# Feed-forward gate and up tiles: one 512-column matmul for two products, corrections summed apart

## The chip, the cores and the metric

The kernel runs on one core of a Trainium2 chip. The metric is the device time of one execution in microseconds. Three runs of the kernel before gave 1154.39 to 1155.62 us, with a median of 1154.85 us. One further execution was profiled; all rows and durations below come from it.

## The reference

Five stages follow each other on a sequence of 256 tokens with 1,024 channels, in float32: two hybrid layers (a gated recurrence, gated linear attention and sparse attention side by side), a feed-forward stage, a mixing stage, and a second feed-forward stage. The change touches the feed-forward stages alone:

```python
def swiglu(x, w_gate, w_up, w_down):
    return (jax.nn.silu(x @ w_gate) * (x @ w_up)) @ w_down

h = h + 0.5 * swiglu(rmsnorm_2(h, ffn1_norm[l]), ffn1_w_gate[l], ffn1_w_up[l], ffn1_w_down[l])
...
h = h + 0.5 * swiglu(rmsnorm_2(h, ffn2_norm[l]), ffn2_w_gate[l], ffn2_w_up[l], ffn2_w_down[l])
```

`w_gate` and `w_up` are 1024 x 2816, `w_down` is 2816 x 1024.

## The kernel before

TensorE multiplies in a reduced form of float32 (`F32R`). To keep the accuracy of float32, each operand is split into a rounded part and its remainder, `hi` and `lo`, and a product is the sum of three: hi by hi, hi by lo and lo by hi. `mm3` (lines 136 to 141) issues these three matmuls into one PSUM region.

The weights come as 362 units of 128 x 1024 values (512 KB), in the order of their use. `weights()` (lines 101 to 114) issues the DMA of a unit into `raw` (3 buffers), casts it to `hi` on ScalarE (line 112) and subtracts on VectorE to get `lo` (line 113); `hi` and `lo` have 5 buffers each. These steps get a high priority, so they stand in their engines' queues as far ahead of the matmuls as the buffers allow.

The activations of a stage, normed and transposed to 128 channels x 8 tiles x 256 tokens, are split in the same way. `norm()` makes two tiles for them, `xh` and `xl`, which `split` (lines 131 to 134) fills.

A projection reads a unit in one of two ways. `proj_a` holds x as the stationary operand and moves 512 columns of weights; its result has tokens on the partitions. `proj_b` (lines 173 to 182) holds 128 x 128 of the weights and moves the 256 tokens; its result has channels on the partitions. For each unit it takes the eight channel tiles `k` in turn and calls `mm3`: 24 matmuls of 256 columns. With n = 2 two units fill one PSUM bank, `ps[:, 0]` and `ps[:, 1]`.

`ffn()` makes the first 512 of the 2,816 hidden channels by `proj_a`, and the other 2,304 in nine turns of `j` (lines 858 to 863). A turn is `g = proj_b("fg")`, `u = proj_b("fu")`, four units in all, then `gated`: a tanh on ScalarE (line 839, tile `fth`), two multiplications on VectorE (lines 841 and 842, tile `fs`), and a split into `hh` and `hl` (lines 133 and 134). `out_proj` multiplies `hh` and `hl` by `w_down` (tiles `op`, 512 columns each).

The PSUM pool `pj` has four banks in rotation, for all projections and for the four accumulators of `out_proj`. A scheduler sets the order on each engine from the order of the program and the priorities; each engine works through its own queue in that order.

Of the kernel before, what the change touches and what calls it, by code (L numbers as in the profile page):

```python
# [8 lines left out]
F32R = mybir.dt.float32r  # L9
U8 = mybir.dt.uint8  # L10
AF = mybir.ActivationFunctionType
ALU = mybir.AluOpType
# [3 lines left out]
P = 128  # L16
S = 256
D = 1024
KT = D // P
# [14 lines left out]
class Net:  # L34
# [138 lines left out]
    def proj_b(self, x, name, n=2):  # L173
# [7 lines left out]
            self.tick()  # L181
        return ps

    def rsqrt(self, out, v, scale, eps, post=None):

        n = v.shape[-1]
        g = self.nc.gpsimd
        g.tensor_scalar(out, v, scale, eps, ALU.mult, ALU.add)
        g.tensor_tensor(out, out, self.mhalf[:, :n], ALU.pow)
        if post is not None:  # L190
            g.tensor_scalar(out, out, post, None, ALU.mult)
# [58 lines left out]
    def norm(self, g_src):  # L250


        g = self.row_bc(g_src, D, "g_bc")
        xh = self.big.tile([P, KT, S], F32R, tag="xh", name="xh")
        xl = self.big.tile([P, KT, S], F32R, tag="xl", name="xl")

        def fill(t):
            with self.tc.high_priority(self.ahead(2 * LEAD)):
                halves = self.normed(t, g)

            def turn():
                for b, xs in enumerate(halves):
                    ps = self.transposes([xs[:, P * k:P * (k + 1)] for k in range(4)], "xT")
                    ks, ts = slice(4 * b, 4 * b + 4), slice(P * t, P * (t + 1))
                    with self.tc.high_priority(self.ahead(2 * LEAD)):
                        self.split(xh[:, ks, ts], xl[:, ks, ts], ps)

            return turn

        return (xh, xl), fill  # L270
# [559 lines left out]
    def ffn(self):  # L830

        nc = self.nc
        x = self.xn
        hh = self.work([P, 22, S], "hh", dtype=F32R)
        hl = self.work([P, 22, S], "hl", dtype=F32R)

        def gated(g, u, n):
            th = self.tmp([P, n], "fth")
            nc.scalar.activation(th, g, AF.Tanh, scale=0.5)
            s = self.tmp([P, n], "fs")  # L840
            nc.vector.scalar_tensor_tensor(s, th, 1.0, g, ALU.add, ALU.mult)
            nc.vector.tensor_tensor(s, s, u, ALU.mult)
            return s

        def transposed(t, s):
            yield
            yield
            tp = self.transposes([s[:, P * i:P * (i + 1)] for i in range(4)], "hT")
            ts = slice(P * t, P * (t + 1))
            self.split(hh[:, 0:4, ts], hl[:, 0:4, ts], tp)  # L850

        gs = []
        self.proj_a(x, "fg", lambda t, ps: gs.append(ps))
        us = self.proj_a(x, "fu")
        for t in range(2):
            self.start(transposed(t, gated(gs[t], us[t], 512)))
        f = lambda z: z.rearrange("p a b -> p (a b)")
        for j in range(9):
            g = self.proj_b(x, "fg")
            u = self.proj_b(x, "fu")  # L860
            s = gated(f(g), f(u), 512)
            ks = slice(4 + 2 * j, 6 + 2 * j)
            self.split(f(hh[:, ks, :]), f(hl[:, ks, :]), s)
        self.join()
        self.out_proj((hh, hl), 22, 0.25)
# [195 lines left out]
def layouts(np, ins):  # L1061
# [31 lines left out]
    def ffn(n):  # L1093
# [4 lines left out]
        return out + rows(wd, range(0, DFF, 256))  # L1098

    units += ffn(1)  # L1100
    w = g("w_in_2")[0]
    units += pa(w, 1024) + pb(w, 0, 1024) + pa(w, 2048) + pa(w, 1536) + pb(g("w_gate_2")[0], 0, 2048)
    for n in ("attn", "gmlp"):
        wb = g(f"w_branch_{n}_2")[0]
        units += [tiles(wb[:, c:c + 256]) for c in range(0, 1024, 256)]
    units += rows(g("w_out_2")[0], range(0, 1024, 256))
    units += ffn(2)

    cols = np.zeros((P, NCOLS), f)
# [70 lines left out]
```

## Time and profile before

| What | Value |
|---|---|
| Median of 3 runs | 1154.85 us |
| Profiled execution | 1154.77 us |
| its span, first to last instruction | 1153.1 us |
| TensorE busy | 1131.9 us, 98% |
| VectorE busy | 776.5 us, 67% |
| ScalarE busy | 590.5 us, 51% |
| Mean granted clock of TensorE | 0.998 |
| Feed-forward stages, turns of j | 624.4 to 728.9 us and 981.8 to 1086.3 us |

The span is the time between the first and the last instruction; the execution is 1.7 us longer. In the rows, PE is TensorE's matmuls, PEld its loads of stationary operands, DVE is VectorE, ACT is ScalarE. The length that a matmul is shown with (283 ns for 256 columns) is a modelled one with its way through the array; matmuls follow each other at a shorter distance, so what one costs is read from the distance of their starts. "L141" is line 141 of the kernel, and `fg<-xh,hi` names the tile written and the tiles read, with buffer numbers left out. Behind "idle before" stands what ended an engine's idle time in front of an instruction.

### The profile page before, as it was taken

What the parts mean: (1) busy time and instruction counts of PE and PEld (TensorE: products, weight loads), DVE (VectorE), ACT (ScalarE), POOL (GpSimd) and SP (SyncE); (2) the same over time, 40 slices, a digit from 0 to 9 for tenths busy, and PEclk for the clock granted to TensorE, in tenths of its full rate; (3) what the DMA queues carried; (4) which work ended last, traced back from release to release, by engine and by line L of the source; (5) the groups of instructions that cost most, each with busy time, mean ns of one, the idle gap of its engine ahead of it and who ended that gap; (6) DMA issues with size and microseconds to landing.
All of it is one profiled execution on the core that took longest, in us unless ns stands there. A gap on an engine that the chain in (4) does not pass through costs nothing.

```text
span 1153.1 us, 18080 instructions
## 1 busy us (share of the span) xinstructions
PE 1131.9 (98%) x7114; PEld 1010.1 (88%) x7114; DVE 776.5 (67%) x1138; ACT 590.5 (51%) x854; POOL 92.4 (8%) x133
## 2 busy tenths in 40 slices
PE   8999999999999999999999999999999999999997
PEld 5888789898798888989878999888989997999986
DVE  5697896886668879678656656546495477656543
ACT  5645745554464675456445444435564445444432
POOL 1111111121011210112100000000020000000000
PEclk9999999999999999999999999999999999999999
DMA  8846555556564654455656566666653665666662
GB/s 271 258 144 201 156 159 156 152 170 179 173 205 148 199 148 142 139 161 166 183 163 222 178 183 184 189 194 203 189 175 105 184 191 179 188 183 183 186 197 74
DMA packets 59309, 203.57 MB, mean 177 GB/s; under 512 B 6668, under 2 KB 9620, under 8 KB 59224
## 3 DMA queue, kind: packets, MB, share of 16 engines
q1 hardware_dynamic: 59224, 202.42, 58.1%
q8 instruction: 56, 0.92, 0.3%
q14 instruction: 29, 0.24, 0.1%
HBM read 201.20 MB, written 2.11 MB: 176 GB/s over the span
## 4 chain that ended last, share of the span: by engine, by line
PE 88%; DVE 6%; DMA 2%; ACT 1%; issue 1%; POOL 0%; SPq 0%; DVEq 0%; POOLq 0%; ACTq 0%
PE op L141 19%; PE fg L141 11%; PE fu L141 11%; PE gatep L141 4%; PE mk L141 4%; PE mq L141 4%; PE mz L141 4%; PE mv L141 3%; PE mo L141 3%; DVE lo L113 2%; PE brp L141 2%; PE qk2p L141 2%; PE dz L141 2%; PE dv L141 2%; DMA raw<-in_w 2%; PE gr L141 1%
## 5 line engine op out<-in xcount | busy, mean ns | idle before, releaser
L113 DVE TENSOR_TENSOR lo<-raw,hi 128x1024 fp32r<-128x1024 f32 x362 | 445.2, 1232 | 278.0 <-ACT hi L112 275.5
L112 ACT CAST hi<-raw 128x1024 fp32r<-128x1024 f32 x362 | 379.0, 1048 | 455.5 <-PE op L141 90.2
L141 PE MATMUL fu<-xh,hi 128*128 128x256 f32 x288 | 81.7, 284 | 0.0
L141 PE MATMUL fg<-xh,lo 128*128 128x256 f32 x288 | 81.5, 283 | 0.0
L141 PE MATMUL fg<-xl,hi 128*128 128x256 f32 x288 | 81.5, 283 | 0.0
L141 PE MATMUL fu<-xh,lo 128*128 128x256 f32 x288 | 81.5, 283 | 0.0
L141 PE MATMUL fg<-xh,hi 128*128 128x256 f32 x288 | 81.5, 283 | 0.0
L141 PE MATMUL fu<-xl,hi 128*128 128x256 f32 x288 | 81.5, 283 | 0.0
L141 PE MATMUL op<-hi,hh 128*128 128x512 f32 x176 | 68.6, 390 | 0.0
L141 PE MATMUL op<-hi,hl 128*128 128x512 f32 x176 | 68.5, 389 | 0.0
L141 PE MATMUL op<-lo,hh 128*128 128x512 f32 x176 | 68.5, 389 | 0.0
L141 PEld LDWEIGHTS fg<-xl,hi 128*128 128x128 f32 x288 | 55.3, 192 | 0.1
L141 PEld LDWEIGHTS fg<-xh,hi 128*128 128x128 f32 x288 | 55.3, 192 | 0.1
L141 PEld LDWEIGHTS fg<-xh,lo 128*128 128x128 f32 x288 | 55.3, 192 | 0.0
L141 PEld LDWEIGHTS fu<-xl,hi 128*128 128x128 f32 x288 | 55.3, 192 | 0.0
L141 PEld LDWEIGHTS fu<-xh,hi 128*128 128x128 f32 x288 | 55.3, 192 | 0.0
L141 PEld LDWEIGHTS fu<-xh,lo 128*128 128x128 f32 x288 | 55.3, 192 | 0.0
L284 POOL TENSOR_TENSOR r<-r,mhalf 128x1 f32<-128x1 f32 x12 | 6.6, 554 | 557.4 <-DVE r L283 557.4
L141 PE MATMUL op<-hi,yh 128*128 128x512 f32 x128 | 51.1, 400 | 0.0
L141 PE MATMUL op<-lo,yh 128*128 128x512 f32 x128 | 50.0, 390 | 0.0
L141 PE MATMUL op<-hi,yl 128*128 128x512 f32 x128 | 49.9, 390 | 0.0
L634 DVE SCALAR_TENSOR_TENSOR cacc<-pad,cols,cacc 128x256 f32<-128x256 f32 x96 | 41.0, 479 | 0.1
(403 smaller groups left out, 2979.1 us busy)
## 6 DMA issues: line engine op xcount, KB each, us to landing
raw<-in_w SPq DMA_DIRECT2D x362, 512.0 KB, 3.6
x<-in_x SPq DMA_DIRECT2D x2, 512.0 KB, 5.4
g_bc<-in_norm_g SPq DMA_DIRECT2D x2, 512.0 KB, 4.4
mlg<-in_ml_norm_g SPq DMA_DIRECT2D x2, 512.0 KB, 5.4
skew<-strips SPq DMA_DIRECT2D x4, 256.0 KB, 5.7
pen<-skew SPq DMA_DIRECT2D x8, 128.0 KB, 3.7
mb<-M SPq DMA_DIRECT2D x2, 512.0 KB, 4.7
g_bc<-in_ffn_norm SPq DMA_DIRECT2D x2, 512.0 KB, 5.2
```

Of the source, the lines that this page charges most:

```text
L112: nc.scalar.copy(hi, raw)
L113: nc.vector.tensor_sub(lo, raw, hi.bitcast(F32))
L141: self.nc.tensor.matmul(out, lhsT=lhsT, rhs=rhs, start=first and i == 0, stop=last and i == 2)
L284: nc.gpsimd.tensor_tensor(r, r, self.mhalf[:, 0:1], ALU.pow)
L634: nc.vector.scalar_tensor_tensor(acc[:, c, :], pad[:, c, 1 + i:1 + i + S], w(i), acc[:, c, :], ALU.mult, ALU.add)
```

## The change

A new function `proj_c` takes the place of `proj_b` for `fg` and `fu` in the turns of j. The two tiles `xh` and `xl` become the halves of one tile `x2`, in which the 256 values of `xh` and the 256 of `xl` of a channel tile lie next to each other. For each k one matmul moves both halves through the weights' `hi` part: 512 columns, which fill one PSUM bank with hi by hi in the first half and hi by lo in the second. A matmul of 256 columns then adds lo by hi to the second half. So a unit has 16 matmuls instead of 24 and a bank of its own, whose second half is the sum of the corrections. ScalarE copies the second half to SBUF, and VectorE adds the first half to it; `gated` reads the result from SBUF (tag `s2`, six buffers of 2 KB a partition).

```diff
+    def proj_c(self, name, out):
+        nc = self.nc
+        for c in range(out.shape[1]):
+            ps = self.acc([P, 2, S], name)
+            wh, wl = self.weights()
+            for k in range(KT):
+                ks = slice(P * k, P * (k + 1))
+                nc.tensor.matmul(ps, lhsT=wh[:, ks], rhs=self.x2[:, k], start=k == 0, stop=False)
+                nc.tensor.matmul(ps[:, 1, :], lhsT=wl[:, ks], rhs=self.x2[:, k, 0, :], start=False, stop=k == KT - 1)
+            self.tick()
+            nc.scalar.copy(out[:, c, :], ps[:, 1, :])
+            nc.vector.tensor_tensor(out[:, c, :], out[:, c, :], ps[:, 0, :], ALU.add)
+        return out
...
-        xh = self.big.tile([P, KT, S], F32R, tag="xh", name="xh")
-        xl = self.big.tile([P, KT, S], F32R, tag="xl", name="xl")
+        self.x2 = self.big.tile([P, KT, 2, S], F32R, tag="x2", name="x2")
+        xh, xl = (self.x2[:, :, i, :] for i in range(2))
...
-            g = self.proj_b(x, "fg")
-            u = self.proj_b(x, "fu")
+            g = self.proj_c("fg", self.work([P, 2, S], "fg", 6, tag="s2"))
+            u = self.proj_c("fu", self.work([P, 2, S], "fu", 6, tag="s2"))
```

The lines behind the new function move by 17: the tanh of line 839 is line 856 after the change, the multiplications of 841 and 842 are 858 and 859. The copy is line 197 and the add line 198.

The order on ScalarE, second turn of j of the first feed-forward stage, before (`hi` is the cast of a weight unit, `fth` the tanh, `hh` the cast of the gated result):

```order
L112 CAST hi_6399<-raw_6397 128x1024
L112 CAST hi_6430<-raw_6428 128x1024
L839 ACTIVATE fth_6359<-fg_6237 128x512
L112 CAST hi_6460<-raw_6458 128x1024
L112 CAST hi_6498<-raw_6496 128x1024
L133 CAST hh_5920<-fs_6361 128x512
```

The same place after the change (`fg_6215`, `fg_6240`, `fu_6266` and `fu_6291` are the PSUM banks of the four units, `fg_6214` and `fu_6265` the SBUF tiles):

```order
L197 COPY fg_6214<-fg_6215 128x256
L112 CAST hi_6378<-raw_6376 128x1024
L197 COPY fg_6214<-fg_6240 128x256
L856 ACTIVATE fth_6316<-fg_6214 128x512
L112 CAST hi_6403<-raw_6401 128x1024
L197 COPY fu_6265<-fu_6266 128x256
L112 CAST hi_6436<-raw_6434 128x1024
L197 COPY fu_6265<-fu_6291 128x256
L112 CAST hi_6461<-raw_6459 128x1024
L133 CAST hh_5917<-fs_6318 128x512
```

A copy stands behind each cast of a weight unit, and the tanh behind the second copy.

The order on VectorE at the same place, before (`lo` is the remainder of a weight unit, `fs` the gated result, `hl` its remainder):

```order
L113 TENSOR_TENSOR lo_6400<-raw_6397,hi_6399 128x1024
L113 TENSOR_TENSOR lo_6431<-raw_6428,hi_6430 128x1024
L841 SCALAR_TENSOR_TENSOR fs_6361<-fth_6359,fg_6237 128x512
L113 TENSOR_TENSOR lo_6461<-raw_6458,hi_6460 128x1024
L842 TENSOR_TENSOR fs_6361<-fs_6361,fu_6298 128x512
L113 TENSOR_TENSOR lo_6499<-raw_6496,hi_6498 128x1024
L134 TENSOR_TENSOR hl_5921<-fs_6361,hh_5920 128x512
```

And after:

```order
L198 TENSOR_TENSOR fg_6214<-fg_6214,fg_6215 128x256
L113 TENSOR_TENSOR lo_6379<-raw_6376,hi_6378 128x1024
L198 TENSOR_TENSOR fg_6214<-fg_6214,fg_6240 128x256
L858 SCALAR_TENSOR_TENSOR fs_6318<-fth_6316,fg_6214 128x512
L113 TENSOR_TENSOR lo_6404<-raw_6401,hi_6403 128x1024
L198 TENSOR_TENSOR fu_6265<-fu_6265,fu_6266 128x256
L113 TENSOR_TENSOR lo_6437<-raw_6434,hi_6436 128x1024
L198 TENSOR_TENSOR fu_6265<-fu_6265,fu_6291 128x256
L859 TENSOR_TENSOR fs_6318<-fs_6318,fu_6265 128x512
L113 TENSOR_TENSOR lo_6462<-raw_6459,hi_6461 128x1024
L134 TENSOR_TENSOR hl_5918<-fs_6318,hh_5917 128x512
```

An add stands behind each `lo`, and the two multiplications follow the second add of `fg` and of `fu`. In both programs the first use of a weight unit, the writes of the x halves and the first matmuls of a stage stand in the same order, with the same semaphores.

## Rows read from the trace of the kernel before

**Rows 1.** The page, part 1: engine, busy us, share of the span, instructions.

```profile
PE 1131.9 (98%) x7114; PEld 1010.1 (88%) x7114; DVE 776.5 (67%) x1138; ACT 590.5 (51%) x854; POOL 92.4 (8%) x133
```

**Rows 2.** The page, part 4: the chain that ended last, by engine, by line.

```profile
PE 88%; DVE 6%; DMA 2%; ACT 1%; issue 1%; POOL 0%; SPq 0%; DVEq 0%; POOLq 0%; ACTq 0%
PE op L141 19%; PE fg L141 11%; PE fu L141 11%; PE gatep L141 4%; PE mk L141 4%; PE mq L141 4%; PE mz L141 4%; PE mv L141 3%; PE mo L141 3%; DVE lo L113 2%; PE brp L141 2%; PE qk2p L141 2%; PE dz L141 2%; PE dv L141 2%; DMA raw<-in_w 2%; PE gr L141 1%
```

**Rows 3.** That chain in order of time: start us, us, what.

```profile
624.55 5.75 PE fg L141 x48
...
633.18 0.87 PE hT L196 x8
...
723.32 5.76 PE fu L141 x48
729.08 55.92 PE op L141 x247
...
981.79 5.75 PE fg L141 x48
```

**Rows 4.** Busy time by window; the columns are in the first line.

```profile
core 0: us, PE busy (x) PEld busy (x) DVE busy (x) ACT busy (x) POOL busy (x), PEclk, DMA share, GB/s
660.00:680.00 20.00, 20.00 (x169) 20.00 (x168) 12.24 (x13) 9.30 (x11) 0.00 (x0) 1.00 0.63 184
740.00:760.00 20.00, 20.00 (x89) 16.54 (x89) 8.65 (x8) 8.28 (x8) 0.00 (x0) 1.00 0.66 187
```

**Rows 5.** Timeline of the gate and up tiles, first and last TensorE matmul used.

```profile
659.80 0.28 PE L141 MATMUL fg<-xh,hi 128*128 128x256 f32 x1
...
667.96 0.28 PE L141 MATMUL fu<-xh,lo 128*128 128x256 f32 x1
```

**Rows 6.** Timeline of the out-projection, first and last TensorE matmul used.

```profile
729.62 0.40 PE L141 MATMUL op<-hi,hh 128*128 128x512 f32 x1
...
749.80 0.39 PE L141 MATMUL op<-lo,hh 128*128 128x512 f32 x1
```

**Rows 7.** ScalarE by line and shape: busy us, mean ns of one, idle before.

```profile
L112 ACT CAST hi<-raw 128x1024 fp32r<-128x1024 f32 x362 | 379.0, 1048 | 455.5 <-PE op L141 90.2 <-issue 66.9 <-DMA raw<-in_w 48.7
...
L839 ACT ACTIVATE fth<-fg 128x512 f32<-128x512 f32 x22 | 13.1, 594 | 2.1 <-PE fg L141 2.0
...
L133 ACT CAST hh<-fs 128x512 fp32r<-128x512 f32 x18 | 11.1, 614 | 0.0
...
L898 ACT ACTIVATE gates<-gatep,bgh 128x256 f32<-128x256 f32 x16 | 6.7, 470 | 0.0
...
L801 ACT COPY at<-gp 128x256 f32<-128x256 f32 x4 | 1.3, 374 | 0.0
```

**Rows 8.** VectorE by line and shape, the same columns.

```profile
L113 DVE TENSOR_TENSOR lo<-raw,hi 128x1024 fp32r<-128x1024 f32 x362 | 445.2, 1232 | 278.0 <-ACT hi L112 275.5 <-PE iq L141 0.9 <-PE fg L141 0.6
...
L842 DVE TENSOR_TENSOR fs<-fs,fu 128x512 f32<-128x512 f32 x22 | 15.1, 687 | 11.2 <-PE fu L141 11.2
L841 DVE SCALAR_TENSOR_TENSOR fs<-fth,fg 128x512 f32<-128x512 f32 x22 | 15.0, 681 | 0.9 <-ACT fth L839 0.9
...
L134 DVE TENSOR_TENSOR hl<-fs,hh 128x512 fp32r<-128x512 f32 x18 | 12.3, 685 | 0.0
...
L689 DVE SCALAR_TENSOR_TENSOR sz_z<-hp,mr,sz_z 128x256 f32<-128x256 f32 x16 | 9.2, 605 | 5.9 <-POOL pad L626 4.2 <-POOL sz_z L685 1.7
...
L939 DVE TENSOR_TENSOR lg<-al,cmask 128x256 f32<-128x256 f32 x4 | 1.6, 419 | 1.2 <-PE al L937 1.2
```

**Rows 9.** Timeline of the gate and up tiles, one ScalarE cast of weights.

```profile
659.92 1.05 ACT L112 CAST hi<-raw 128x1024 fp32r<-128x1024 f32 x1 [1.83 <-PE fu L141]
```

**Rows 10.** TensorE's waits: us in total, times, longest us.

```profile
PE fg L141 <- ACT xh L133: 0.5, 2, 0.3
PE fg L141 <- DVE xl L134: 0.5, 2, 0.2
```

**Rows 11.** The page, part 5: a group of TensorE's loads of stationary operands.

```profile
L141 PEld LDWEIGHTS fg<-xl,hi 128*128 128x128 f32 x288 | 55.3, 192 | 0.1
```

## The prediction

> **What bounds the kernel now.** I began with the busy shares [rows 1]: TensorE is busy 98% of the span, VectorE 67%, ScalarE 51%. The reader is to see which engine has no room, and which have. The shares of the chain that ended last [rows 2] say the same by another way: 88% of it is TensorE's, and the gate and up tiles (fg, fu) are 22% of it. The chain in order of time [rows 3] is then read for the stage that the change touches: from 624.55 to 729.08 us it holds TensorE's work alone, 5.76 us for each pair of weight units (48 matmuls), but for 0.87 us of eight transposes. The second feed-forward stage has the same pieces (the first at 981.79). Last the stage's own stretch [rows 4]: TensorE busy 20.00 of 20 us, VectorE 12.24, ScalarE 9.30, DMA share 0.63, granted clock 1.00, the 2.4 GHz level. So in this stage time is the number of matmuls by their spacing, and every other engine may grow as long as it stays out of TensorE's way.
>
> **TensorE's part: what is removed.** In the stretch of 256-column matmuls the starts at 659.80 and 667.96 are 68 steps apart [rows 5]: 8.16 / 68 = 0.1200 us. In the out-projection the 512-column starts at 729.62 and 749.80 are 89 steps apart [rows 6]: 20.18 / 89 = 0.2267 us. Both stretches have another stationary tile for each matmul, and neither waits. Twice the columns cost 106.7 ns more, so 256 columns cost 106.7 ns and 13.3 ns are left in either case: a price per matmul, whatever its width.
>
> Before, a unit is 24 matmuls of 256 columns: 24 x 0.1200 = 2.880 us (half of the 5.76 in [rows 3]). After, it is 8 of 512 and 8 of 256 columns, the same 6,144 columns in 16 instructions: 8 x 0.2267 + 8 x 0.1200 = 2.774 us. That is 0.106 us a unit, 8 times 13.3 ns. A feed-forward stage has 9 x 4 = 36 such units, the kernel 72: 72 x 0.106 = 7.6 us. The two widths standing in turn is what no row shows. Bounds: if a wide matmul in this mix costs two narrow ones (0.240), nothing is gained; if the narrow one behind a wide one shows none of its 13.3 ns, 72 x 8 x 13.3 ns = 7.7 us more are gained. I take the spacing that each width has by itself, since the stretches around it are steady to the hundredth over 68 and 89 steps.
>
> A rule of the Trainium skill speaks against this size. Its page "TensorE: Matmul & The Clock Gate", section "Back-to-back issue gap", gives a gap of N / 2.4 + 2.5 ns at the full clock, a fixed part of 2.5 ns where the rows here have 13.3. By that rule the eight matmuls saved would give 20 ns a unit and 1.4 us in all, 1153.4 us. The rows of both widths disagree with it (it would give 109 and 216 ns), so it has a small chance below.
>
> **What is added on ScalarE and VectorE.** Each unit gets a ScalarE copy of 128x256 from PSUM and a VectorE add of 128x256 with one operand in PSUM. The nearest rows are 374 ns (at<-gp; 470 for gates<-gatep, which has a bias) [rows 7] and 419 ns (lg<-al,cmask; 605 for the slowest row of that shape) [rows 8]. I take the first of each, copies and adds of the same kinds of operands: 72 x 0.374 = 26.9 us on ScalarE, 72 x 0.419 = 30.2 us on VectorE. The tanh and the two multiplications read SBUF instead of PSUM; VectorE's rows of 512 columns lie between 681 and 687 ns either way, and I cost that at nothing.
>
> All of it lies beside TensorE. Per turn of j (four units, 11.1 us) VectorE has 4 x 1.232 (lo) + 4 x 0.419 + 0.681 + 0.687 + 0.685 = 8.7 us, ScalarE 4 x 1.048 (hi) + 4 x 0.374 + 0.594 + 0.614 = 6.9 us. With the slow ends (0.470, 0.605) it would be 9.4 and 7.3 us. There is room on both, so the queues catch up in each turn.
>
> What this hides behind is checked at the waits. New is that ScalarE's tanh waits for VectorE's second add of fg, and that add stands behind a lo, which stands behind a hi that ScalarE starts only when TensorE leaves a unit (before: 1.83 us of idle until then [rows 9]). Following the order that the change section shows from the end of fg's second unit: hi to 1.05, copy to 1.45, lo 1.08 to 2.31, add to 2.73, tanh to 3.33, and only then the hi that could have begun at 2.77. Behind the waiting tanh stand hi casts that TensorE needs four units, 11 us, later, since five pairs of weight tiles are held. The delay of 0.6 us is made good within the turn.
>
> The PSUM banks: before, a gate or up tile of two units had one bank; now each unit has one, of the same four. A unit must be read out before the fourth unit after it starts, 3 x 2.77 = 8.3 us after its end. The slowest is fg's first unit, whose add waits behind lo and hl: about 3.4 us. At the hand-over to the out-projection, the last fu unit's add ends about 2.7 us after the unit; the matmul that needs that bank comes 2.72 + 3 x 0.227 = 3.4 us after it. A miss would cost tenths of a microsecond, twice.
>
> **The joined x tile.** Both halves stand interleaved in one tile instead of two. Their writers keep their shape (four runs of 128 columns), and stationary reads stay 128 neighbouring columns. Should the first matmuls of a stage now have to wait for the write of both halves, it would cost at most one VectorE write of 685 ns [rows 8] in each of five norms, 3.4 us; the waits on these writes are 0.5 us each now [rows 10]. The order shows the same semaphores at the same matmuls, so I take nothing. Weights are asked for every 2.77 us instead of 2.88; the out-projection asks for one every 2.72 us, and TensorE is busy 20.00 of 20 there [rows 4].
>
> **Sum.** The profiled execution took 1154.77 us (span 1153.1 and 1.7 around it), the median is 1154.85. 1154.85 - 7.6 = 1147.2 us.
>
> **Rivals.**
> - No gain: the 13.3 ns belongs to something that the wider matmul keeps, and a wide one in this mix costs what two narrow ones do, 0.240 us. For: the wide rows come from a stage with other operands (there the weights move and x is stationary). Against: two stages give the same remainder. Time 1154.8. The rule of the Trainium skill that was weighed above ends in the same band.
> - Slower: weight loads. A load is shown with 192 ns [rows 11] while narrow matmuls come every 120, so loads overlap each other now, and loading is busy 20.00 of 20 us [rows 4]. If the load for a wide matmul can't start before the narrow one in front of it does, and can't run beside that one's own load, it shows 192 - 120 = 72 ns each: 576 x 72 ns = 41.5 us, less the 7.6, 1188.8 us. It turns to a loss from 13.3 ns for each wide matmul on. Against: each of the narrow matmuls now has just this load in front of it and keeps 0.120.
> - More gain: the narrow matmul's load has had the whole wide one to hide under, and its 13.3 ns goes too: 1139.5 us. For: loading has idle time as soon as matmuls are wide (16.54 of 20) [rows 4]. Against: the wide matmuls there keep their 13.3 ns all the same.
>
> **How the numbers follow.** The forecast has 0.82, with its own range 1145.5 to 1149 (a few tenths of a microsecond at the hand-overs and stage starts, up to the 3.4 us of the joined tile thinly, and 0.6 us by which the three runs differ). No gain has 0.08, slower 0.04, more gain 0.06. About 0.2%, 2.3 us, is what a measurement can tell from no change; so faster is 0.82 + 0.06 = 0.88, same 0.08, slower 0.04. The range 1145 to 1150 takes the forecast and a part of the joined tile's bound, and leaves out less than 2 in 10.
>
> **What would show it.** Right: starts within a unit are 0.227 and 0.120 us apart in turn, a turn of j takes 11.1 instead of 11.52 us, TensorE stays at 20.00 of 20, VectorE rises to about 15.6 and ScalarE to about 12.4 of 20. Wrong: gaps of TensorE that end on a VectorE add (banks), on hi or lo (weights), or a wide spacing of 0.240 or more. If the gain is there and the sum is not, the stage starts after the norms are the place to look.

## The result, and the profile after

The changed kernel took 1147.29 us in the median of four runs (1146.36 to 1148.72), beside 1155.15 us (1154.39 to 1155.62) for four runs of the kernel before: a ratio of 0.9939, with a 95% interval of 0.9925 to 0.9952. It is faster, by 7.9 us, and 1147.2 us had been predicted. The profiled execution took 1147.36 us, with a span of 1145.7 us.

Part 1 of the page, and the first of the chain's lines in part 4, answer to [rows 1, 2]:

```profile
PE 1126.8 (98%) x6538; PEld 978.7 (85%) x6538; DVE 801.8 (70%) x1210; ACT 610.4 (53%) x926; POOL 94.5 (8%) x133
...
PE 92%; DVE 4%; ACT 1%; issue 1%; DMA 1%; POOL 0%; SPq 0%; DVEq 0%; POOLq 0%; ACTq 0%
```

TensorE has 576 matmuls fewer (72 units x 8) and is as full as before. VectorE and ScalarE have 72 instructions more each. The change has taken work from the engine that sets the time and given work to two that don't.

Busy time by window, with the columns of [rows 4], whose two windows these are:

```profile
660.00:680.00 20.00, 20.00 (x118) 17.47 (x116) 14.57 (x20) 11.91 (x19) 0.00 (x0) 1.00 0.60 185
740.00:760.00 20.00, 20.00 (x90) 16.55 (x89) 8.68 (x8) 8.21 (x8) 0.00 (x0) 1.00 0.64 189
```

In the gate and up tiles TensorE is still at 20.00 of 20. The load of stationary operands, which filled its 20 us before, has idle time now (17.47). VectorE went from 12.24 to 14.57, ScalarE from 9.30 to 11.91.

The timeline of TensorE's matmuls, for comparison with [rows 5]; the first four lines are of the first feed-forward stage, the last two of the second:

```profile
659.66 0.39 PE L194 MATMUL fg<-x,hi 128*128 128x512 f32 x1
659.89 0.27 PE L195 MATMUL fg<-x,lo 128*128 128x256 f32 x1
...
667.98 0.39 PE L194 MATMUL fg<-x,hi 128*128 128x512 f32 x1
...
670.75 0.39 PE L194 MATMUL fg<-x,hi 128*128 128x512 f32 x1
...
999.97 0.40 PE L194 MATMUL fg<-x,hi 128*128 128x512 f32 x1
...
1003.51 0.40 PE L194 MATMUL fg<-x,hi 128*128 128x512 f32 x1
```

From 659.66 to 667.98 there are 24 pairs of a wide and a narrow matmul: 8.32 / 24 = 0.3467 us, the sum of 0.2267 and 0.1200 that was worked out. The two parts differ from that: a narrow matmul starts 0.23 us behind its wide one (659.66 to 659.89), and the next wide one 0.115 us behind that, so only the pair follows the sum. From 659.66 to 670.75 is one turn of j, 11.09 us instead of 11.52. From 999.97 to 1003.51 there are ten pairs, and they take 0.354 us each. This second spacing was not predicted; it comes back below.

The groups of ScalarE and VectorE that answer to [rows 7, 8]; the columns are the same:

```profile
L113 DVE TENSOR_TENSOR lo<-raw,hi 128x1024 fp32r<-128x1024 f32 x362 | 445.3, 1232 | 243.0 <-ACT hi L112 241.8
...
L198 DVE TENSOR_TENSOR fg<-fg 128x256 f32<-128x256 f32 x36 | 14.9, 414 | 0.0
```

```profile
L856 ACT ACTIVATE fth<-fg 128x512 f32<-128x512 f32 x22 | 13.8, 626 | 26.4 <-DVE fg L198 24.4 <-PE fg L141 2.1
L197 ACT COPY fg<-fg 128x256 f32<-128x256 f32 x36 | 13.2, 366 | 0.0
L197 ACT COPY fu<-fu 128x256 f32<-128x256 f32 x36 | 13.2, 366 | 0.0
L133 ACT CAST hh<-fs 128x512 fp32r<-128x512 f32 x18 | 11.0, 614 | 0.0
```

The new copies take 366 ns and the new adds 414. The tanh now waits for the add of line 198, 24.4 us in all, where its waits were 2.1 us before [rows 7]; this costs nothing, as the queue around it shows. The timeline of VectorE, then of ScalarE, in the turn of j that begins at 656.9 us:

```profile
662.61 0.41 DVE L198 TENSOR_TENSOR fg<-fg 128x256 f32<-128x256 f32 x1
663.64 1.23 DVE L113 TENSOR_TENSOR lo<-raw,hi 128x1024 fp32r<-128x1024 f32 x1 [0.61 <-ACT hi L112]
664.78 0.41 DVE L198 TENSOR_TENSOR fg<-fg 128x256 f32<-128x256 f32 x1
```

```profile
662.56 1.05 ACT L112 CAST hi<-raw 128x1024 fp32r<-128x1024 f32 x1 [0.93 <-ACT fg L197]
663.51 0.37 ACT L197 COPY fg<-fg 128x256 f32<-128x256 f32 x1
665.23 0.63 ACT L856 ACTIVATE fth<-fg 128x512 f32<-128x512 f32 x1 [1.35 <-DVE fg L198]
665.77 1.03 ACT L112 CAST hi<-raw 128x1024 fp32r<-128x1024 f32 x1
```

The second unit of fg begins at 659.66 and is eight pairs, 2.77 us, long: it ends at 662.43. Hi, copy, lo, add and tanh follow each other, and the tanh starts 2.80 us behind the unit. The next hi starts 3.34 us behind it, where 2.77 would have done. TensorE has no idle time in this whole stage.

### The profile page after: what moved, and what is told of

Read it like the earlier page. It is cut to its first block, busy times and chain, and to the rows that moved or that the text cites. A ratio compares the mean times of both kernels' runs of the same rounds, so it can differ in the third digit from the quotient of the medians.

```text
span 1145.7 us, 17056 instructions
## 1 busy us (share of the span) xinstructions
PE 1126.8 (98%) x6538; PEld 978.7 (85%) x6538; DVE 801.8 (70%) x1210; ACT 610.4 (53%) x926; POOL 94.5 (8%) x133
## 4 chain that ended last, share of the span: by engine, by line
PE 92%; DVE 4%; ACT 1%; issue 1%; DMA 1%; POOL 0%; SPq 0%; DVEq 0%; POOLq 0%; ACTq 0%
PE op L141 19%; PE fg L194 6%; PE fu L194 6%; PE gatep L141 4%; PE mk L141 4%; PE mq L141 4%; PE mz L141 4%; PE fg L195 3%; PE fu L195 3%; PE mo L141 3%; PE mv L141 3%; PE brp L141 2%; PE qk2p L141 2%; PE dz L141 2%; PE iq L141 2%; PE dk L141 2%
## 5 line engine op out<-in xcount | busy, mean ns | idle before, releaser
L194 PE MATMUL fu<-x,hi 128*128 128x512 f32 x288 | 101.9, 397 | 0.0
L194 PE MATMUL fg<-x,hi 128*128 128x512 f32 x288 | 101.7, 396 | 0.0
L195 PE MATMUL fg<-x,lo 128*128 128x256 f32 x288 | 80.4, 279 | 0.0
L195 PE MATMUL fu<-x,lo 128*128 128x256 f32 x288 | 80.4, 279 | 0.0
L194 PEld LDWEIGHTS fg<-x,hi 128*128 128x128 f32 x288 | 54.1, 188 | 13.0
L194 PEld LDWEIGHTS fu<-x,hi 128*128 128x128 f32 x288 | 54.1, 188 | 12.9
L195 PEld LDWEIGHTS fg<-x,lo 128*128 128x128 f32 x288 | 54.3, 188 | 0.1
L195 PEld LDWEIGHTS fu<-x,lo 128*128 128x128 f32 x288 | 54.2, 188 | 0.0
L141 PE MATMUL mq<-x,hi 128*128 128x256 f32 x256 | 48.2, 289 | 0.0
L141 PE MATMUL gatep<-x,hi 128*128 128x256 f32 x256 | 47.3, 286 | 0.0
```

The lines of the kernel that those rows point to most:

```text
L141: self.nc.tensor.matmul(out, lhsT=lhsT, rhs=rhs, start=first and i == 0, stop=last and i == 2)
L194: nc.tensor.matmul(ps, lhsT=wh[:, ks], rhs=self.x2[:, k], start=k == 0, stop=False)
L195: nc.tensor.matmul(ps[:, 1, :], lhsT=wl[:, ks], rhs=self.x2[:, k, 0, :], start=False, stop=k == KT - 1)
```

## Where the 7.9 us are

The first profiles of the two kernels differ at two places. The table takes two starts from the timeline of each profiled kernel: the first matmul of fg in the turns of j of the first feed-forward stage, narrow or wide, and the last of the kernel's matmuls. What lies between holds the turns of j of both feed-forward stages and the mix stage; what lies ahead, the layers above all, has the same projections in all rows of this table. The kernels other than the two first are told of in the next section.

| Kernel | first fg of the turns | last matmul | between |
|---|---|---|---|
| before | 624.39 | 1145.81 | 521.42 |
| before, a second profile | 621.80 | 1143.25 | 521.45 |
| joined x tile alone | 622.99 | 1144.43 | 521.44 |
| changed, but three narrow matmuls | 622.19 | 1143.69 | 521.50 |
| changed | 622.58 | 1138.39 | 515.81 |
| changed, a second profile | 622.97 | 1137.06 | 514.09 |
| wide and narrow in groups | 627.74 | 1142.92 | 515.18 |
| changed, and the mix stage too | 621.34 | 1133.98 | 512.64 |

Without wide matmuls, 521.4 to 521.5 us lie between, to a tenth of a microsecond. With them it is 5.6 us less in one profile and 7.4 us less in the other. The starts of the first column move by 2.6 us between two profiles of the kernel before, and by 6.4 us over the eight rows. So the 1.8 us by which the changed kernel was ahead there (624.39 to 622.58) can't be put down to the change.

## The experiments

**The joined x tile alone.** The kernel before with `x2` in place of `xh` and `xl`, the projections as they were.

```diff
-        xh = self.big.tile([P, KT, S], F32R, tag="xh", name="xh")
-        xl = self.big.tile([P, KT, S], F32R, tag="xl", name="xl")
+        self.x2 = self.big.tile([P, KT, 2, S], F32R, tag="x2", name="x2")
+        xh, xl = (self.x2[:, :, i, :] for i in range(2))
```

> The joined x tile alone: both halves in one tile, gate and up tiles still in 24 narrow matmuls of 256 columns. Theory A (only the matmuls' number counts, the joined tile costs nothing): within 1 us of the kernel before, pairs of units 5.76 us long, stage starts as before. Theory B (the 1.8 us by which the changed kernel reached the feed-forward stage earlier, in unchanged lines, come from the joined tile): 1.5 to 2 us faster than before, already at the start of the first feed-forward stage. Theory C (first matmuls of a stage wait for both halves): up to 3.4 us slower.

Measured: 1154.07 us beside 1155.43, a ratio of 0.999 (0.998 to 1.000). The layout costs nothing in the feed-forward stages, by the table; a gain in the layers of up to 0.2% can't be told from their scatter. Its turns of j start 1.4 us earlier than in the first profile of the kernel before, nearly as theory B has it, but 1.2 us later than in the second (622.99, 624.39 and 621.80), where x has two tiles.

**The changed kernel with narrow matmuls.** Everything of the change but the wide matmul.

```diff
-                nc.tensor.matmul(ps, lhsT=wh[:, ks], rhs=self.x2[:, k], start=k == 0, stop=False)
+                nc.tensor.matmul(ps[:, 0, :], lhsT=wh[:, ks], rhs=self.x2[:, k, 0, :], start=k == 0, stop=False)
+                nc.tensor.matmul(ps[:, 1, :], lhsT=wh[:, ks], rhs=self.x2[:, k, 1, :], start=False, stop=False)
```

> The new sums alone: a bank for each unit, corrections summed apart, copy by ScalarE and add by VectorE, but with three narrow matmuls for each k, 24 in a unit, as before. Theory A (copies and adds lie wholly beside TensorE): the time of the kernel before, within 1 us; 20.00 of 20 us TensorE in the stage; VectorE about 15 and ScalarE about 11.5 of 20. Rival (the read-out costs something that the fewer matmuls hid): 1 us or more slower than before, with gaps of TensorE that end on a VectorE add.

Measured: 1154.82 us beside 1155.43, a ratio of 0.9996 (0.9983 to 1.0008). Its timeline shows the three matmuls of one channel tile and the first of the next; the second view is of the window that was read above:

```profile
659.76 0.28 PE L194 MATMUL fg<-x,hi 128*128 128x256 f32 x1
659.88 0.28 PE L195 MATMUL fg<-x,hi 128*128 128x256 f32 x1
660.00 0.28 PE L196 MATMUL fg<-x,lo 128*128 128x256 f32 x1
660.12 0.28 PE L194 MATMUL fg<-x,hi 128*128 128x256 f32 x1
```

```profile
660.00:680.00 20.00, 20.00 (x169) 20.00 (x168) 14.40 (x21) 11.30 (x18) 0.00 (x0) 1.00 0.63 187
```

The spacing is 0.12 us, as before. VectorE and ScalarE carry the 2.2 and 2.0 us that were added to them, and TensorE has no gap. So the copies, adds, banks and the wait of the tanh are free here, and the gain is all the wide matmul's. The second matmul, which has the same stationary operand as the first, is no cheaper than the third, and the trace has a load for it all the same (168 loads beside 169 matmuls in the window). So a wide matmul saves a matmul together with its load, and no run here takes the two apart.

**The groups.** In the changed kernel, first all eight wide matmuls of a unit, then its eight narrow ones.

```diff
             for k in range(KT):
-                ks = slice(P * k, P * (k + 1))
-                nc.tensor.matmul(ps, lhsT=wh[:, ks], rhs=self.x2[:, k], start=k == 0, stop=False)
+                nc.tensor.matmul(ps, lhsT=wh[:, ks[k]], rhs=self.x2[:, k], start=k == 0, stop=False)
+            for k in range(KT):
```

> The changed kernel with the eight wide matmuls of a unit first and the eight narrow ones behind them, so that the width changes twice in a unit instead of sixteen times. In the changed kernel's trace a pair takes 0.3467 us in most of the first feed-forward stage and 0.3533 in the second. Theory D (the 6.7 ns more are paid where a wide matmul follows a narrow one, by the way the two streams lie to each other): no unit over 2.79 us in either stage, up to 2 us faster than the changed kernel. Rival (the 6.7 ns belong to the wide matmul or to the stage, in whatever order): the second stage keeps units of 2.82 us, same time as the changed kernel.

Measured: 1146.87 us, a ratio of 0.9928 (0.9911 to 0.9944), the same as the changed kernel on that chip (below). The profiled execution was the longest of its six, 1151.88 us, by its layers; its feed-forward stages can be read. The timeline, with one row for each group:

```profile
656.52 2.00 PE L194 MATMUL fu<-x,hi 128*128 128x512 f32 x8
658.36 1.12 PE L196 MATMUL fu<-x,lo 128*128 128x256 f32 x8
659.31 2.00 PE L194 MATMUL fu<-x,hi 128*128 128x512 f32 x8
```

Eight wide matmuls take 1.84 us, 0.230 each, and eight narrow ones 0.95, 0.119 each: 2.79 us a unit. A unit is shorter than the 2.88 us of narrow matmuls in this order too, but a wide matmul is not exactly 0.2267 us here. All units of both stages have 2.79 us, but for the first of a stage (2.77) and the one behind the transposes (2.88). So theory D is right that the 2.82 is gone from the second stage; the up to 2 us that it gave can't be seen, with 515.18 us in the table beside 515.81 and 514.09 for the changed kernel.

**The changed kernel once more**, on the same chip as the three above.

> The changed kernel once more, unaltered, beside the others on one chip. If the longer pair (0.3533 us) is a matter of how the stream of matmuls starts in an execution, another execution shows it in other stretches, and the runs spread over 2 us or so; if it belongs to the second stage by its addresses or its order, this profile shows 0.3467 and 0.3533 in the same places. About 7.5 us faster than before by either.

Measured: 1147.30 us (1145.58 to 1150.35), a ratio of 0.9931 (0.9915 to 0.9947). Against the run with narrow matmuls it is 1154.82 - 1147.30 = 7.5 us, for the wide matmul alone, give or take some 2 us by the intervals of the two. Its timeline at the place in the second feed-forward stage that was shown above:

```profile
1000.11 0.40 PE L194 MATMUL fg<-x,hi 128*128 128x512 f32 x1
...
1003.57 0.40 PE L194 MATMUL fg<-x,hi 128*128 128x512 f32 x1
```

Here ten pairs take 3.46 us, not 3.54. The program is the same to the last instruction, and the spacing another.

**The kernel before, a second profile.**

> The kernel before, profiled a second time, to see how far its stage starts move by themselves. Theory A (the 1.8 us by which the first feed-forward turn starts earlier in the changed kernel is scatter of the layer stages): the second matmul stage positions differ from the first profile's (mo 119.9 us, mq 138.8, first narrow gate matmul 624.4) by 1 us or more, towards 118.5, 137.0 and 622.6. Theory B (it belongs to the joined tile of x): they stay within 0.3 us of 119.9, 138.8 and 624.4. In both the pair of feed-forward stages keeps 104.5 us for its gate and up turns.

Measured: 1152.21 us in its one run, the first narrow fg at 621.80 us. That is theory A for these two executions. TensorE's waits from 55 to 155 us show where the layers scatter. The kernel before in its first profile, and in its second:

```profile
PE pTp L196 <- ACT X L760: 1.9, 1, 1.9
PE dv L141 <- DVE ks L517: 0.7, 1, 0.7
PE gp L798 <- DVE X L764: 0.7, 1, 0.7
PE pTp L196 <- DVE lg L570: 0.6, 1, 0.6
```

```profile
PE pTp L196 <- ACT X L760: 0.9, 1, 0.9
PE gp L798 <- DVE X L764: 0.7, 1, 0.7
```

3.9 us of waits in the one and 1.6 in the other, all in the first layer, where TensorE, VectorE and ScalarE hand small pieces to each other. The changed kernel's first profile has 2.2 us there. The profile of the groups, whose layers are those of the changed kernel, has 3.6 us, and behind them its granted clock was at half for some microseconds; its turns of j start latest in the table. Its window from 130 us, where both profiles of the kernel before have a clock of 1.00:

```profile
130.00:134.00 4.00, 4.00 (x16) 3.10 (x15) 1.82 (x3) 1.52 (x4) 0.00 (x0) 0.50 0.69 221
```

**The same form in the mix stage too.** Another 24 units, q and k and the gates.

```diff
-            ps = self.proj_b(x, "gatep")
+            self.proj_c("gatep", gt[:, 2 * u:2 * u + 2, :])
...
-                nc.scalar.activation(gt[:, j, :], ps[:, c, :], AF.Tanh, scale=0.5, bias=bh[:, j:j + 1])
+                nc.scalar.activation(gt[:, j, :], gt[:, j, :], AF.Tanh, scale=0.5, bias=bh[:, j:j + 1])
```

> The changed kernel, with the same form of projection in the mix stage too: its 8 units of q and k and 16 of the gates have the wide matmul, the correction apart, and a copy and an add per unit. Theory A (each unit of 24 narrow matmuls gives back what 8 of the 13.3 ns fixed prices cost, 0.106 us, wherever TensorE sets the pace): 24 x 0.106 = 2.5 us less than the changed kernel's 1147.3, so 1144.8. Rival (VectorE and ScalarE, which hold attention and the spatial gate beside this stage, 20 and 15 of 26 us at 822 to 848, deliver the weight halves or the tanh of the gates late): 1147 or more, with idle of TensorE before gatep or brp. Rival (the longer of the two spacings, 0.3533 us, which gives 0.053 us a unit): 1146.0.

Measured: 1145.42 us beside 1153.24, a ratio of 0.9926 (0.9910 to 0.9942). By time alone this can't be told from the changed kernel's 0.9931; by the stages it can. The mix stage up to its out-projection took 144.94 us before (790.17 to 935.11) and in the changed kernel (784.69 to 929.63), and takes 143.51 here (783.44 to 926.95): 1.4 us less, between the 1.3 of the longer spacing and the 2.5 of the shorter. Both are in its timeline, the longer in q and k, the shorter in the last eight units of the gates:

```profile
804.87 0.40 PE L194 MATMUL qk2p<-x,hi 128*128 128x512 f32 x1
...
805.93 0.40 PE L194 MATMUL qk2p<-x,hi 128*128 128x512 f32 x1
...
889.71 0.40 PE L194 MATMUL gatep<-x,hi 128*128 128x512 f32 x1
...
890.75 0.39 PE L194 MATMUL gatep<-x,hi 128*128 128x512 f32 x1
```

Three pairs take 1.06 us in the one and 1.04 in the other. This version has the lowest ratio of all that were run, but its interval holds the ratios of the changed kernel and of the groups too; what is clear is the 1.4 us in the mix stage of the profile.

**And in the layers.** The same in 56 more units, the layers' iq, gq, gk, dz, mq and mk; once with widths in turn, once in groups.

```diff
-        nc.scalar.mul(gqk[:, 0], self.proj_b(x, "gq"), 0.125)
-        nc.scalar.copy(gqk[:, 1], self.proj_b(x, "gk"))
+        self.proj_c("gq", gqk[:, 0], 0.125)
+        self.proj_c("gk", gqk[:, 1])
```

> As the run before, and in the two hybrid layers also every projection of this shape but the 4-row one: 28 units a layer (iq, gq, gk, dz, mq, mk). Theory A (TensorE sets the pace in the layers too): another 56 x 0.106 = 5.9 us, so 1138.9. Rival (VectorE is the bound there: 9.88 us busy of 10 at 80 to 90, 13.82 ScalarE and 14.00 VectorE-bound weight loads beside it, and each unit adds a 0.41 us add and a 0.37 us copy, 23 and 20 us in all): the gain of the layers is lost where VectorE is full; with a third of the adds on the path 23/3 = 7.7 us more, 1146.6, slower than the run before, with TensorE waiting for lo in the layers.

> As the run before, with the 8 wide matmuls of a unit ahead of its 8 narrow ones instead of alternating. Theory A (the price goes by the matmul, not by the order): the same as the run before within 0.2%, 1138.9. Rival (the longer spacing of a pair, 0.3533 us, comes of alternating widths, and is gone when they are grouped): up to 152 units x 8 x 0.0067 = 8.1 us less if all units of the run before had it, about half of that if half of them had. Rival (in a group the units run at 2.79 us, as a grouped unit showed, against 2.774): 152 x 0.016 = 2.4 us more.

Measured: 1157.05 us, a ratio of 1.0038 (1.0024 to 1.0052), and in groups 1154.89 us, 1.0016 (1.0005 to 1.0027). Both are slower than the version with the mix stage, by 11.6 and 9.5 us, and theory A of the first expectation is wrong for the layers. The groups are 2.2 us ahead of the widths in turn, less than the 4 to 8 us of the rival that the longer spacing gives; what of it is the order and what the layers' scatter was not taken apart. (Of the busy times in the first expectation, 13.82 us of 14 is VectorE at 137 to 151 us in the changed kernel; the 9.88 of 10 at 80 to 90 and the 14.00 are TensorE's loads. VectorE is at 10.00 of 10 there.) The largest cause is not the one that was expected. From the run with widths in turn, the largest wait of TensorE from 20 to 640 us, then its matmuls at the first of the two:

```profile
PE gk L194 <- DVE ks L537: 9.5, 2, 5.7
```

```profile
68.27 0.80 PE L194 MATMUL gk<-x,hi 128*128 128x512 f32 x1 [5.74 <-DVE ks L537]
...
69.51 0.41 PE L195 MATMUL gk<-x,lo 128*128 128x256 f32 x1
69.72 0.63 PE L194 MATMUL gk<-x,hi 128*128 128x512 f32 x1
70.15 0.41 PE L195 MATMUL gk<-x,lo 128*128 128x256 f32 x1
70.36 0.63 PE L194 MATMUL gk<-x,hi 128*128 128x512 f32 x1
```

gk does not use ks. It waits for a PSUM bank: of four, two hold dk, which is free only when ks has been computed from it, and gq, which took one bank for its two units, now takes the other two. In the kernel before it is dv that comes next for dk's first bank, and it waits for ks 0.7 us in the first profile (above). Behind the wait of gk a pair takes 0.64 us instead of 0.35. Two windows of that stretch (columns as above) tell why:

```profile
64.00:66.00 2.00, 0.00 (x0) 0.00 (x0) 2.00 (x7) 0.00 (x0) 0.00 (x0) 1.00 0.30 47
...
70.00:72.00 2.00, 2.00 (x7) 1.68 (x7) 0.82 (x2) 0.00 (x0) 1.40 (x2) 0.50 0.31 47
```

The granted clock is 0.50, the 1.2 GHz level, behind 5.7 us without a matmul.

**Two tests of that cause.** The form in the mix stage and in iq and dz alone; and in everything but gq and gk.

```diff
-        self.proj_c("gq", gqk[:, 0], 0.125)
-        self.proj_c("gk", gqk[:, 1])
+        nc.scalar.mul(gqk[:, 0], self.proj_b(x, "gq"), 0.125)
+        nc.scalar.copy(gqk[:, 1], self.proj_b(x, "gk"))
```

> The kernel with the form in the mix stage, and beside it in the 16 units of iq and dz of the two layers, whose results nobody needs at once. Theory (TensorE sets the pace there, each unit is worth 0.053 us at the longer spacing of a pair and 0.106 at the shorter): 0.8 to 1.7 us less than that kernel, a ratio to the kernel before of 0.9912 to 0.9919. Rival (VectorE, 14.00 us busy of 14 at 76 to 90 in the first layer, where dz stands, loses 16 x 0.41 = 6.6 us to the adds): a ratio of 0.993 to 0.998, with TensorE waiting for lo or W in the layers.

> The kernel with the form in all projections of the layers, with gq and gk alone put back to narrow matmuls and one bank for two units. Theory A (what made that kernel slower is the PSUM banks: four accumulators, two of them dk's until its normalisation has read them, and gq and gk now take four in place of two, so that gk waits 5.7 and 3.8 us for ks, and TensorE's granted clock is at half speed for some 6 us behind that): both waits are gone, 9.5 us, and the half clock with them, some 3 us by 66 to 73; of the 1157.05 some 1144.5 is left, a ratio of 0.9925. Rival (VectorE's added adds, 20 of whose 23 us remain): 1154 to 1156, a ratio of 1.001 to 1.003.

Measured: 1148.32 us, a ratio of 0.9946 (0.9932 to 0.9961) for the first, 1151.46 us, 0.9972 (0.9962 to 0.9983), for the second. Putting gq and gk back takes the ratio from 1.0038 to 0.9972, some 7.6 us, of the 12.5 that theory A gave. The waits on ks are gone, and others stand in the layers. TensorE's largest waits from 20 to 640 us in the second of the two kernels:

```profile
PE gv L141 <- DVE dzs L199: 3.8, 3, 2.3
PE st L668 <- DVE qk L657: 2.5, 2, 1.3
...
PE nd L675 <- DVE W L671: 1.2, 2, 0.6
```

gv waits for a bank that dz's new add on VectorE gives back late, and st and nd wait for results of VectorE, which they did not in the kernel before. Here the added work of VectorE is on the path, as the rival said, if at a smaller price. These three waits are 7.5 us in all, and the kernel with the form in the mix stage alone has none of them. So theory A covers some 7.6 of its 12.5 us. The profiled execution is the longest of that kernel's twelve (1153.77 us), in part for another reason: it has the longer spacing of a pair in both feed-forward stages.

The first of the two kernels falls into the rival's band of 0.993 to 0.998, and it has 2.5 us of the same wait of gv (not one for lo or W, as the rival had it). In its profile the first iq unit also starts 2.3 us later than in the kernel before (28.51 us for 26.20). The edit touches nothing ahead of that unit. TensorE's granted clock was low there, in the first projection, where the kernel before has 1.00 (the profile of the groups has 0.62 from 12 to 16 us):

```profile
12.00:16.00 4.00, 3.30 (x12) 2.27 (x11) 4.00 (x10) 3.06 (x4) 0.76 (x1) 0.60 0.97 259
16.00:20.00 4.00, 4.00 (x11) 3.12 (x11) 2.09 (x2) 0.78 (x1) 0.00 (x0) 0.55 0.86 270
```

## Why the prediction was right

- **The price per matmul.** Right, and the whole of the gain: with all else of the change in place and narrow matmuls, nothing was gained (1154.82); with wide ones, 7.5 us by the medians, and 5.6 and 7.4 us in the two profiles, of the 7.6 predicted. The prediction says of both of its stretches that each matmul has another stationary tile. In the narrow one this does not hold: hi by hi and hi by lo share a tile, and it is loaded twice. What both stretches have is a load for each matmul (7114 of each [rows 1]), so the 13.3 ns may belong to the matmul or to its load.
- **The spacing of the mixed pair.** Taken as 0.2267 + 0.1200 us. This is one of two values that were seen. The first feed-forward stage has it behind the transposes of its first turn; the three units ahead of them take 0.353. In the first profile the second stage keeps the 0.353 to its end; in the second profile it has 0.3467 behind its transposes as well. So in the first profile the sum is too large for 39 units, by 39 x 8 pairs x 0.0067 = 2.1 us of the 7.6: 5.5 us remain, and 5.6 were found. In the second it is so for 6 units, 0.3 us: 7.3 remain, and 7.4 were found.
- **Where the rest of the 7.9 us is from.** Not predicted: layers that were not changed differ by 2.6 us between two profiles of the kernel before, and by 6.4 us over the eight rows of the table, where the longest had a half clock on its way. The first profile of the kernel before was the second longest. So the exactness of 1147.2 is owed in part to chance. The prediction allowed 0.6 us for the runs' differences, half of the 1.2 us between its three; some 3 us each way is what the layers call for.
- **Copies, adds, and the wait of the tanh.** Right in kind and nearly in size: 366 ns for 374, 414 for 419 (the mean of the 36 of a tile), a tanh from 2.80 to 3.43 us behind its unit where 2.73 to 3.33 was worked out. The tanh itself is 0.63 us, not 594 ns, now that it reads SBUF (the mean of 626 ns holds four of 22 that still read PSUM); this is hidden too. ScalarE and VectorE were put at 12.4 and 15.6 of 20 us and are at 11.9 and 14.6. The sums added whole durations, and in the trace an instruction begins shortly before the one ahead of it ends (lo from 663.64 for 1.23 us, the add behind it at 664.78).
- **Banks.** Right: the add on fg's first unit ends at 663.02, 3.4 us after that unit (659.66), and no matmul waits. The layers show that this was not self-evident: there the same form waited for banks 5.7 us at one place.
- **The joined tile.** Right within the scatter: 521.44 us against 521.42.
- **Rivals.** *Weight loads*: fallen; a pair would have taken 0.419 us, and the loads have less to do than before (17.47 of 20). *No gain* and *more gain*: fallen; a pair takes 0.3467 or 0.3533 us, not 0.360 and not 0.333. The rule of the Trainium skill that stood beside the first of them ("TensorE: Matmul & The Clock Gate", section "Back-to-back issue gap") would make a pair 0.325 us. The same section calls that gap the one of a single matmul, and gives some 131 ns for 512 columns in a stream. The trace agrees with neither, at 0.227 to 0.237 us from a 512-column matmul to the next start.

What stays open is why the same instructions run at one of two spacings. The program alone does not settle it, since two executions of one program differ; groups have a third value, 0.349 a pair, in both stages. In the six profiles with the widths in turn, the first three units of all twelve feed-forward stages have the longer spacing. Behind the eight transposes of the first turn nine stages have the shorter and three the longer, each to its end. Nothing was run that sets it.

## What to carry to other kernels

Where TensorE is full and each matmul comes with a load of its stationary operand, count matmuls, not columns alone: two narrow ones that share their stationary operand can be one wide one, if their sums may stand apart, and the price of the matmul saved is read from the difference of two widths in the trace. The extra reading of PSUM is free only where the other engines have room and the banks come back in time: the same edit gained in the feed-forward and mix stages and lost in the layers, so look at the next user of each bank, and then at the engines' busy shares. Before a gain of a fraction of a percent is put down to a stage, profile the kernel before twice, compare stage by stage, and read the granted clock of each stretch.

## What was not expected of the hardware

- The pair of a 512- and a 256-column matmul has two steady spacings, 0.3467 and 0.353 us, in executions of one program, and in stages of one execution; a stretch of wide ones in a unit of its own has 0.230 each, where the out-projection has 0.2267 [rows 6].
- A matmul whose stationary operand is the same as that of the one in front of it was no cheaper: 0.12 us, all three, each with a load of its own.
- The tanh of 128x512 took 0.63 us from SBUF and 594 ns from PSUM [rows 7].
- TensorE idle for 5.7 us came back at half its clock, and its first pairs took 0.64 us instead of 0.35: a wait cost more than its length. The clock also fell in layers whose projections no edit had touched, to 0.50 from 130 to 134 us in one profile.
